# A new order for the pooling mixer and the entry of the second feed-forward network

## The chip, the cores and the metric

The kernel runs on one core of a Trainium2 chip. The core has a matrix engine (TensorE, PE in the profile), a vector engine (VectorE, DVE), an activation engine (ScalarE, ACT), GpSimd (POOL) and SyncE (SP), which issues transfers. Each engine executes its own list of instructions in the order in which the program wrote them and waits on semaphores of the others. The metric is the device time of one launch in microseconds.

## The reference

Two layers of a streaming trunk run over 32 sample tokens and 512 prompt tokens that share weights, in float32. Layer 0 is an attention and recurrence mixer, layer 1 a pooling mixer, and each is followed by a SwiGLU feed-forward network (FFN).

```python
def swiglu(x, w_gate, w_up, w_down):
    return (jax.nn.silu(x @ w_gate) * (x @ w_up)) @ w_down
...
def pool_mixer(xn, buf, start_pos, pool_w, pool_scale):
    b, t, _ = xn.shape
    xcat = jnp.concatenate([buf.astype(xn.dtype), xn], axis=1)
    xf = xcat.astype(jnp.float32)
    cs = jnp.concatenate([jnp.zeros((b, 1, D_MODEL), jnp.float32), jnp.cumsum(xf, axis=1)], axis=1)
    pos = start_pos + jnp.arange(t)
    outs = []
    for gi, win in enumerate(POOL_WINDOWS):
        sl = slice(gi * POOL_GROUP, (gi + 1) * POOL_GROUP)
        end = cs[:, POOL_BUF + 1:POOL_BUF + 1 + t, sl]
        begin = cs[:, POOL_BUF + 1 - win:POOL_BUF + 1 - win + t, sl]
        cnt = jnp.minimum(win, pos + 1).astype(jnp.float32)[None, :, None]
        outs.append((end - begin) / cnt - xf[:, POOL_BUF:, sl])
    d = jnp.stack(outs, axis=2)
    y = jnp.einsum('btgc,gcd->btgd', d, pool_w.astype(jnp.float32)).reshape(b, t, D_MODEL)
    y = y * pool_scale.astype(jnp.float32)
    return y.astype(xn.dtype), xcat[:, -POOL_BUF:]
...
        x = x + y
        x = x + swiglu(rmsnorm(x, norm_ffn[layer]), ffn_gate[layer], ffn_up[layer], ffn_down[layer]).astype(x.dtype)
```

D_MODEL is 1024, the hidden width D_FF 2816, the pooling windows are 2, 4, 8 and 16 tokens, and 15 normalised tokens of history are kept.

## The kernel before

**Layout.** The residual x stays in SBUF with features on the partitions: 8 tiles of 128 features by 544 tokens, used as two halves of 272 tokens (`HALVES`). A float32 product is three matmuls of split operands: high by high, high by low, low by high. So each weight block and each activation tile is first split into a high part (an ACT copy) and a low part (a DVE subtraction).

**FFN.** The hidden width is done in 11 pairs of 128-wide blocks (`PAIRS`). A pair is a Strassen-like scheme (`strassen`): 7 products, each for gate and up, so 14 steps, instead of 8; its right sides are the forms b11, n1, n2, t3, b21, t4 and b22 of the normalised x (sums and differences of feature and token halves), its left sides sums of weight blocks. `beat.tick` counts steps, and `beat.later(n, f)` issues f n steps on. `last_down` multiplies the last hidden blocks by the down weights, adds to x tile by tile and calls `after0(m)`, which makes the mixer's split copies of tile m. The first pair of the second FFN is the exception: it is computed by `plain`, without Strassen, so that it needs only tile k of x and weight blocks a11, a12, a21 and a22 for its step `mm(i, us, k)`; `gate_out` and `up_out` close it.

**Pooling mixer.** `into(t, i)` multiplies token block t (six of them) by the pooling weights of half i of the features into a PSUM bank (12 matmuls). `mid` scales such a bank by the token's 1/rms `rt` into `ptm` (or `pts` for the last block, the 32 sample tokens), by turns on ACT and DVE. `pool_out(m)` applies the window as a banded matrix with 12 matmuls into two PSUM banks and has DVE add both to tile m of x. `pool_hist` prepares the history of the sample stream (a transposition, a DVE copy `hist`, 16 matmuls, two ACT copies into `pts`), `pool_state` writes the new history out (`so`).

**Forms of the second FFN.** `LateForms.add(m)` makes tile m's high parts and its square on ACT; the DVE part (`low`: two low parts, the square added to `nacc`) is issued at the next tile. After all eight tiles `sums()` makes the forms n1, n2, t3 and t4 in ten pieces. `scales` sums the squares over the partitions (`rs`) and takes the root, `n3.out` spreads 1/rms over the partitions through PE and an ACT copy (L204).

**Weights.** `Supply` holds a list of loads, splits and additions with due times in beats; `ahead` issues what is due while slots are free, `need(n)` issues the list up to the block n. Loads go through SP's queue, second summands of weight sums through POOL's.

**Order.** PE, DVE, ACT and SP run exactly in program order here. PSUM has two banks each of `sm` (function `small`) and `z`, and four of `one`.

Of the kernel before, what the change touches and what calls it, by code (L numbers as in the profile page):

```python
# [31 lines left out]
def kernel(  # L32
# [174 lines left out]
    class Norm:  # L207
# [24 lines left out]
        def add(self, k):  # L232
            self.split(k)
            self.square(k)
# [84 lines left out]
    class LateForms(Forms):  # L319
# [10 lines left out]
        def tmp2(self, i):  # L330
            return [hp.tile([P, T], F32R if i > 3 else F32, tag=f"h{p}{i}", name=nm("tmp")) for p in "hl"]

        def add(self, k):

            g = col(self.gcol + k)
            bs = [(x[:, k, s], *self.block(k, h)) for h, s in HALVES]
            for src, h, _ in bs:
                ac.activation(h, src, AF.Copy, scale=g)
            t = self.acc if k == 0 else s2.tile([P, T + NS], F32, tag="nsq", name=nm("nsq"), bufs=1)[:, :T]
            ac.activation(t, x[:, k], AF.Square)  # L340

            def low():
                for src, h, l in bs:
                    ve.scalar_tensor_tensor(l, src, g, h.bitcast(F32), op0=ALU.mult, op1=ALU.subtract)
                if k:
                    ve.tensor_add(self.acc, self.acc, t)

            return low

        def sums(self):  # L350
            g = lambda k: col(self.gcol + k)
            two = lambda t: t.rearrange("p (j c) -> p j c", j=2)
            d, t, q = [[two(b) for b in self.tmp2(i)] for i in range(3)]
            J = range(4)
            at = lambda b, j: b[j // 2][:, j % 2]

            def high(n, i, src):
                ac.activation(self.form(n)[0][:, 2 * i : 2 * i + 2], src, AF.Copy, scale=-1.0)

            def low(n, i, src):  # L360
                h, l = [b[:, 2 * i : 2 * i + 2] for b in self.form(n)]
                ve.scalar_tensor_tensor(l, src, -1.0, h.bitcast(F32), op0=ALU.mult, op1=ALU.subtract)

            def n1(j):
                ac.activation(self.form("n1")[0][:, j], at(d, j), AF.Copy, scale=g(j))
                ac.activation(at(t, j), x[:, 4 + j, HN:], AF.Copy, scale=g(4 + j))

            def n1_low(j):
                h, l = [b[:, j] for b in self.form("n1")]
                ve.scalar_tensor_tensor(l, at(d, j), g(j), h.bitcast(F32), op0=ALU.mult, op1=ALU.subtract)  # L370

            def value(out, a, sc, b, op):
                ve.scalar_tensor_tensor(out, a, sc, b, op0=ALU.mult, op1=op)

            out = []
            for i in range(2):
                def diff(i=i):
                    ve.tensor_tensor(d[i], x[:, 2 * i : 2 * i + 2, :HN], x[:, 2 * i : 2 * i + 2, HN:], op=ALU.subtract)
                    n1(2 * i)
                    n1(2 * i + 1)  # L380
                out.append(diff)
            for i in range(2):
                out.append(lambda i=i: [n1_low(j) for j in (2 * i, 2 * i + 1)])
            for vals, n, b in (
                (lambda j: value(at(q, j), at(d, j), g(j), at(t, j), ALU.add), "n2", q),
                (lambda j: value(at(d, j), x[:, j, HN:], g(j), at(t, j), ALU.subtract), "t3", d),
                (lambda j: value(at(q, j), x[:, 4 + j, :HN], g(4 + j), at(q, j), ALU.subtract), "t4", q),
            ):
                for i in range(2):
                    def both(i=i, vals=vals, n=n, b=b):  # L390
                        vals(2 * i)
                        vals(2 * i + 1)
                        high(n, i, b[i])
                    out.append(both)
                for i in range(2):
                    out.append(lambda i=i, n=n, b=b: low(n, i, b[i]))
            return out


    warm = accp()  # L400
# [452 lines left out]
    class Supply:  # L853
# [93 lines left out]
            self.split(10, n("t4"), n("t4"))  # L947

        def plain(self, fp):
            for j, (t0, t1) in enumerate(((-20, -12), (-18, -10), (-6, 2), (-2, 5))):  # L950
                n = f"a{j // 2 + 1}{j % 2 + 1}", fp
                self.blocks(t0, n, (2 * fp + j // 2, j % 2))
                self.split(t1, n, n)
# [278 lines left out]
    def pool_hist(i):  # L1232
        pw, hraw = pool["w"], pool["hraw"]
        if not i:
            ph = small()
            pe.transpose(ph[:, :120], hraw[:120, :P], ident[:120, :120])
            ve.tensor_copy(hist, ph[:, :120].rearrange("p (t k) -> p k t", k=KD))
            ptb.append(slot("pts"))
# [28 lines left out]
    queues = {ET.PE, ET.DVE, ET.Activation, ET.SP}  # L1267
    with tc.manual_schedule(engines=queues):
        ffn(supply, n1[0], after0, {(0, 3): lambda: scales(n1[0]), (0, 7): lambda: n1[0].out(), **{(2 * g + 2, 4): lambda g=g: bands(g) for g in range(4)},
                                    (PAIRS - 1, 7): pool_load}, lambda: [pool_hist(i) for i in range(2)])  # L1270


    n2 = n2[0]
# [38 lines left out]
    low = []  # L1312

    def pool_out(m):
        g, i = m // 2, m // 4
# [12 lines left out]
        for h, pp in enumerate((pa, pb)):  # L1328
            xs = x[:, m, h * HN : (h + 1) * HN]
            ve.scalar_tensor_tensor(xs, pp[:, :HN], col(40 + m), xs, op0=ALU.mult, op1=ALU.add)  # L1330
        if low:
            low.pop()()
        low.append(n3.add(m))

    with tc.manual_schedule(engines=queues):
        supply = Supply(1, plain=True)
        for _ in range(2):
            supply.ops.pop(0)[2]()
        banks = {}
# [18 lines left out]
        into(3, 1)  # L1358
        mid((2, 1))
        into(4, 1)  # L1360
        pool_out(1)
        mid((3, 1))
        into(5, 1)
        pool_out(2)
        mid((4, 1), (5, 1))
        supply.need(("a12", 0))
        pool_out(3)
        first = {}
        mm, gate_out, up_out = plain(supply, n3, first)
        for m in range(4, KD + 4):  # L1370
            if m < KD:
                pool_out(m)
                if m in (4, 6):
                    pool_state(m == 6)
                if m == 7:
                    give(*ptm, *ptb)
            elif low:
                low.pop()()
                sums = n3.sums()
            beat.tick(supply)  # L1380
            mm(0, (0, 1), m - 4, lambda: one("f0"))
            if m == KD + 3:
                sums.pop(0)()
                sums.pop(0)()
        for k in range(KD):
            if k % 2 == 0:
                beat.tick(supply)
            mm(1, (0,), k, lambda: small("z"))
            sums.pop(0)()
            if k == 2:  # L1390
                scales(n3)
        n3.out()
        for k in range(KD):
            if k % 2 == 0:
                beat.tick(supply)
            if k == 1:
                gate_out(0)
            if k == 4:
                up_out(0)
            mm(1, (1,), k, small)  # L1400
            if sums:
                sums.pop(0)()
        gate_out(1)
        beat.later(3, lambda: up_out(1))

# [98 lines left out]
```

## Time and profile before

| what | us |
|---|---|
| median of 3 runs (1083.84 to 1087.59) | 1085.4 |
| the profiled execution | 1085.57 |
| its span in the trace | 1083.9 |
| PE busy with matmuls (96% of the span) | 1042.1 |
| DVE busy (70%) | 760.1 |
| ACT busy (45%) | 488.8 |
| POOL busy (19%) | 205.5 |

The mean granted clock of TensorE is 0.984 of full speed. A position in the trace is counted in us from the span's start; the end of the first FFN, the pooling mixer and the plain pair of the second FFN lie between 613 and 724. In rows a bracket says how long the engine was idle before, and what released it.

### The profile page before, as it was taken

What the parts mean: (1) busy time and instruction counts of PE and PEld (TensorE: products, weight loads), DVE (VectorE), ACT (ScalarE), POOL (GpSimd) and SP (SyncE); (2) the same over time, 40 slices, a digit from 0 to 9 for tenths busy, and PEclk for the clock granted to TensorE, in tenths of its full rate; (3) what the DMA queues carried; (4) which work ended last, traced back from release to release, by engine and by line L of the source; (5) the groups of instructions that cost most, each with busy time, mean ns of one, the idle gap of its engine ahead of it and who ended that gap; (6) DMA issues with size and microseconds to landing.
All of it is one profiled execution on the core that took longest, in us unless ns stands there. A gap on an engine that the chain in (4) does not pass through costs nothing.

```text
span 1083.9 us, 19767 instructions
## 1 busy us (share of the span) xinstructions
PE 1042.1 (96%) x7995; PEld 1001.6 (92%) x7995; DVE 760.1 (70%) x1222; ACT 488.8 (45%) x814; POOL 205.5 (19%) x327
## 2 busy tenths in 40 slices
PE   7979999999899999999999999879999999999997
PEld 7978888899899999999999898879999999999986
DVE  6776665767788776767766664878867766677653
ACT  7555554544544444433443344564424434244432
POOL 5162225101611111101010101101101111010100
PEclk9989999999999999999999999889999999999999
DMA  8412213423787467665586313336755676656702
GB/s 225 142 51 69 69 42 110 101 59 89 144 188 153 91 136 175 157 143 118 112 172 156 117 31 68 83 79 148 156 118 123 137 175 148 134 128 118 212 3 83
DMA packets 207787, 129.08 MB, mean 119 GB/s; under 512 B 7127, under 2 KB 192703, under 8 KB 207696
## 3 DMA queue, kind: packets, MB, share of 16 engines
q1 hardware_dynamic: 161472, 102.58, 33.4%
q0 software_dynamic: 45584, 24.11, 17.1%
q8 instruction: 63, 1.03, 0.4%
q10 hardware_dynamic: 640, 1.12, 0.3%
q14 instruction: 28, 0.23, 0.1%
HBM read 123.19 MB, written 4.60 MB: 118 GB/s over the span
## 4 chain that ended last, share of the span: by engine, by line
PE 77%; DVE 9%; issue 5%; ACT 4%; DMA 2%; POOL 2%; ACTq 0%; SPq 0%; DVEq 0%; POOLq 0%
PE xy L1054 28%; PE sm L1115 17%; PE z L1054 11%; PE acc L168 10%; PE ps L1137 2%; DVE la L903 2%; ACT ha L902 1%; DVE sB L554 1%; PE pi L1292 1%; DMA rt<-in_ffn_up_dram 1%; DMA sB<-in_x_prompt_dram 1%; PE sm L1016 1%; POOL sA L573 1%; ACT y L1445 1%; DVE y L1451 1%
## 5 line engine op out<-in xcount | busy, mean ns | idle before, releaser
L1115 PE MATMUL sm<-hh,h 128*128 128x272 f32 x576 | 167.5, 291 | 0.8
L1115 PE MATMUL sm<-hl,h 128*128 128x272 f32 x576 | 165.6, 288 | 0.0
L1115 PE MATMUL sm<-hh,l 128*128 128x272 f32 x576 | 165.5, 287 | 0.0
L916 POOL DMA_DIRECT2D rt<-in_ffn_gate_dram x42 | 54.4, 1296 | 574.9 <-DMA rt<-in_ffn_gate_dram 341.5
L903 DVE TENSOR_TENSOR lt<-rt,ht 128x1024 fp32r<-128x1024 f32 x84 | 103.0, 1227 | 46.9 <-ACT ht L902 46.7
L1115 PEld LDWEIGHTS sm<-hh,h 128*128 128x128 f32 x576 | 108.4, 188 | 4.3 <-DVE x L1118 4.3
L1115 PEld LDWEIGHTS sm<-hh,l 128*128 128x128 f32 x576 | 108.4, 188 | 0.0
L1115 PEld LDWEIGHTS sm<-hl,h 128*128 128x128 f32 x576 | 108.4, 188 | 0.0
L98 ACT ACTIVATE s<-s 128x544 f32<-128x544 f32 x44 | 29.0, 659 | 173.3 <-DVE s L1063 171.0
L903 DVE TENSOR_TENSOR la<-ra,ha 128x1024 fp32r<-128x1024 f32 x67 | 82.0, 1226 | 26.2 <-ACT ha L902 26.2
L1054 PE MATMUL xy<-b,ha 128*128 128x272 f32 x672 | 98.3, 289 | 0.8 <-DVE x L758 0.8
L902 ACT ACTIVATE ht<-rt 128x1024 fp32r<-128x1024 f32 x84 | 88.2, 1050 | 5.5 <-DMA rt<-in_ffn_up_dram 3.2
L1054 PEld LDWEIGHTS xy<-b,ha 128*128 128x128 f32 x672 | 89.6, 188 | 1.0 <-DVE x L758 1.0
L1118 DVE TENSOR_TENSOR x<-x,sm 128x272 f32<-128x272 f32 x160 | 69.2, 433 | 28.9 <-PE sm L1115 27.9
L168 PE MATMUL acc<-xh,whi 128*128 128x272 f32 x320 | 75.0, 316 | 2.2 <-ACT xh L98 2.2
L916 POOL DMA_DIRECT2D rt<-in_ffn_up_dram x42 | 74.8, 1781 | 1.5 <-DMA rt<-in_ffn_up_dram 0.8
L999 ACT ACTIVATE hh<-u 128x544 fp32r<-128x544 f32 x44 | 29.0, 658 | 95.3 <-DVE u L1085 48.2
L168 PE MATMUL acc<-xl,whi 128*128 128x272 f32 x320 | 68.1, 294 | 0.8 <-DVE xl L228 0.8
L902 ACT ACTIVATE ha<-ra 128x1024 fp32r<-128x1024 f32 x67 | 68.6, 1051 | 0.0
L168 PE MATMUL acc<-xh,wlo 128*128 128x272 f32 x320 | 67.7, 293 | 0.0
L168 PEld LDWEIGHTS acc<-xh,whi 128*128 128x128 f32 x320 | 50.2, 192 | 9.3 <-issue 5.7
L1072 ACT ACTIVATE c<-xy 128x272 f32<-128x272 f32 x42 | 16.7, 398 | 87.4 <-PE xy L1054 87.4
(423 smaller groups left out, 2552.3 us busy)
## 6 DMA issues: line engine op xcount, KB each, us to landing
r<-in_ffn_down_dram SPq DMA_DIRECT2D x44, 512.0 KB, 5.6
ra<-in_ffn_gate_dram SPq DMA_DIRECT2D x67, 256.0 KB, 5.7
ra<-in_ffn_up_dram SPq DMA_DIRECT2D x67, 256.0 KB, 6.1
rt<-in_ffn_gate_dram SPq DMA_DIRECT2D x42, 256.0 KB, 3.2
rt<-in_ffn_up_dram SPq DMA_DIRECT2D x42, 256.0 KB, 4.1
rt<-in_ffn_gate_dram POOLq DMA_DIRECT2D x42, 256.0 KB, 5.8
rt<-in_ffn_up_dram POOLq DMA_DIRECT2D x42, 256.0 KB, 7.4
raw<-in_hyb_w_in_dram SPq DMA_DIRECT2D x20, 512.0 KB, 3.7
```

What stands on the lines that cost most here:

```text
L98: i = ac.activation(*a, **k).ins
L168: pe.matmul(ps[:, h, : s.stop - s.start], lhsT=a[:, wi, :], rhs=b[:, s], start=first and j == 0, stop=last and j == 2)
L554: ve.tensor_tensor_scan(r, r, r, 1.0, op0=ALU.mult, op1=ALU.min)
L902: ac.activation(hi, raw, AF.Copy)
L903: ve.tensor_tensor(lo, raw, hi.bitcast(F32), op=ALU.subtract)
L916: gp.dma_start(v(t)[:, u], w, accum_op=ALU.add)
L999: beat.later(n, lambda: ac.activation(a, t, AF.Copy))
L1054: pe.matmul(o, lhsT=lt, rhs=r, start=first and n == 0, stop=n == 11, skip_group_check=True)
L1072: ac.activation(pc, o, AF.Copy)
L1115: pe.matmul(ps, lhsT=lt[:, c], rhs=r[:, s], start=i == 0 and j == 0, stop=i == len(fs) - 1 and j == 2)
L1118: ve.tensor_add(xs, xs, ps)
L1137: pe.matmul(o, lhsT=lt[:, c], rhs=r[:, s], start=i == 0 and j == 0, stop=i == len(fs) - 1 and j == 2, skip_group_check=True)
```

## The change

No arithmetic is added or removed on PE, whose instructions are the same in another order. First, the history's transposition and its copy come before product 12 of the last pair; the 16 matmuls stay behind product 13. Second, the splits of weight blocks a11, a12, a21 and a22 are due earlier: a11's and a12's are issued ahead of the mixer's first `into`, a21's and a22's among the mixer's blocks. Third, `mid` takes the first half's blocks in the order 3, 4, 0, 1, 2, 5, and `pool_state` comes at tiles 1 and 2 with a bank of `one`. Fourth, `mm(0, ...)` of the plain pair follows each `pool_out` from tile 3 on. Fifth, the forms are made tile by tile: `after(n, f)` puts a piece n tiles later, `due()` issues what has come up; the squares have two buffers of their own by turns, and n2, t3 and t4 come piece by piece (`sum`) in a loop of 11 steps, in whose step 2 `scales` stands and in step 4 `n3.out`.

```diff
-        def add(self, k):
+        def add(self, k, at):
...
-            t = self.acc if k == 0 else s2.tile([P, T + NS], F32, tag="nsq", name=nm("nsq"), bufs=1)[:, :T]
-            ac.activation(t, x[:, k], AF.Square)
+            sq = self.acc if k == 0 else hp.tile([P, T], F32, tag=f"h{'hl'[k % 2]}0", name=nm("nsq"))
+            ac.activation(sq, x[:, k], AF.Square)
...
-            return low
-
-        def sums(self):
+            at(1, low)
+            if k < 4:
+                h, l = [b[:, j] for b in self.form("n1")]
+                at(1, lambda: ve.tensor_tensor(d, x[:, k, :HN], x[:, k, HN:], op=ALU.subtract))
+                at(2, lambda: ac.activation(h, d, AF.Copy, scale=gk))
+                at(3, lambda: ve.scalar_tensor_tensor(l, d, gk, h.bitcast(F32), op0=ALU.mult, op1=ALU.subtract))
+            else:
+                at(1, lambda: ac.activation(t, x[:, k, HN:], AF.Copy, scale=gk))
+
+        def sum(self, n, i, at):
...
+            at(0, value)
+            at(1, lambda: ac.activation(h, o, AF.Copy, scale=-1.0))
+            at(2, lambda: ve.scalar_tensor_tensor(l, o, -1.0, h.bitcast(F32), op0=ALU.mult, op1=ALU.subtract))
...
-            for j, (t0, t1) in enumerate(((-20, -12), (-18, -10), (-6, 2), (-2, 5))):
+            for j, (t0, t1) in enumerate(((-20, -12), (-18, -10), (-9, -5), (-8, -4))):
...
-                                    (PAIRS - 1, 7): pool_load}, lambda: [pool_hist(i) for i in range(2)])
+                                    (PAIRS - 1, 7): pool_load,
+                                    (PAIRS - 1, 12): lambda: pool_hist(0)}, lambda: [pool_hist(i) for i in (1, 2)])
...
-        pq = small()
+        pq = one("pq")
...
-        if low:
-            low.pop()()
-        low.append(n3.add(m))
+        due()
+        n3.add(m, after)
...
+        supply.need(("a12", 0))
+        for _ in range(2):
+            supply.ops.pop(0)[2]()
...
-        mid(*[(t, 0) for t in range(6)])
+        mid(*[(t, 0) for t in (3, 4, 0, 1, 2, 5)])
+        supply.need(("a21", 0))
         into(1, 1)
         into(2, 1)
         mid((0, 1), (1, 1))
-        pool_out(0)
...
+        supply.need(("a22", 0))
+        for m in range(KD):
+            pool_out(m)
+            if m < 3:
+                into(m + 3, 1)
+                mid((m + 2, 1))
+                if m:
+                    pool_state(m - 1)
+            else:
+                if m == 3:
+                    mid((5, 1))
+                    first = {}
+                    mm, gate_out, up_out = plain(supply, n3, first)
+                beat.tick(supply)
+                mm(0, (0, 1), m - 3, lambda: one("f0"))
+        give(*ptm, *ptb)
+
+        n3.sum("n2", 0, lambda n, f: after(n + 1, f))
+        n3.sum("n2", 1, lambda n, f: after(n + 3, f))
+        for i, n in enumerate(("t3", "t3", "t4", "t4")):
+            n3.sum(n, i % 2, lambda n, f, i=i: after((5, 6, 10, 12)[i] + n, f))
+        after(6, lambda: gate_out(0))
+        after(9, lambda: gate_out(1))
+        after(9, lambda: up_out(0))
+        for m in range(11):
+            if m == 2:
+                scales(n3)
+            if m == 4:
+                n3.out()
+            due()
             beat.tick(supply)
...
+            if m < 3:
+                mm(0, (0, 1), 5 + m, lambda: one("f0"))
+            else:
+                for k in range(2 * m - 6, 2 * m - 4):
+                    mm(1, (k // 8,), k % 8, small if k > 7 else lambda: small("z"))
```

The first place is PE's list at the end of the last pair of the first FFN. The z products are products 12 and 13, `ident,hraw` is the transposition of the history, and `pw,hist` its matmuls. Before:

```order
L1054 MATMUL xy_7043<-t_459_2967,la_1032_7162 128x272 x4
L1054 MATMUL z_7058<-b_461_2971,ht_1035_7195 128x272 x8
L1054 MATMUL z_7058<-b_461_2971,lt_1036_7196 128x272 x4
L1054 MATMUL z_7078<-b_461_2971,ht_1035_7195 128x272 x8
L1054 MATMUL z_7078<-b_461_2971,lt_1036_7196 128x272 x4
L1236 MATMUL sm_7404<-ident,hraw 128x120 [waits DMASW5_49,DVE_49]
L1241 MATMUL sm_7408<-pw_7215,hist 15x256 [waits DMASW2_49,DVE_49]
L1241 MATMUL sm_7408<-pw_7215,hist 15x256
```

And now:

```order
L1037 MATMUL xy_7043<-t_459_2967,la_1032_7162 128x272 x4
L1219 MATMUL sm_7370<-ident,hraw 128x120 [waits DMASW5_49,DVE_49]
L1037 MATMUL z_7058<-b_461_2971,ht_1035_7195 128x272 x8
L1037 MATMUL z_7058<-b_461_2971,lt_1036_7196 128x272 x4
L1037 MATMUL z_7078<-b_461_2971,ht_1035_7195 128x272 x8
L1037 MATMUL z_7078<-b_461_2971,lt_1036_7196 128x272 x4
L1227 MATMUL sm_7408<-pw_7215,hist 15x256 [waits DMASW2_49,DVE_49]
L1227 MATMUL sm_7408<-pw_7215,hist 15x256
```

The transposition has moved ahead of both products, so that one product pair stands between it and the first matmul that needs its copy.

The second place is ACT's list around tile 3 of the pooling mixer. L338 rows are high parts of a tile of x (`b`, `tmp`), L340 its square, L1300 (L1287 now) a `mid`, and L902 the high part of a weight block (`ha`). Before:

```order
L338 ACTIVATE b_1120_7880<-x,cols 128x272 [waits DVE_49]
L338 ACTIVATE tmp_7957<-x,cols 128x272 [waits DVE_49]
L340 ACTIVATE nsq_7961<-x 128x544 [waits DVE_49]
L1300 ACTIVATE ptm_7717<-pi_7901,rt_7814 63x512 [waits PE_49]
L902 ACTIVATE ha_1135_7965<-ra_1105_7721 128x1024 [waits DMAHW1_49,DMAHW0_49]
L902 ACTIVATE ha_1137_7969<-ra_1106_7724 128x1024 [waits DMAHW3_49,DMAHW2_49]
L338 ACTIVATE b_1120_7880<-x,cols 128x272 [waits DVE_49]
L338 ACTIVATE tmp_7957<-x,cols 128x272 [waits DVE_49]
L340 ACTIVATE nsq_7988<-x 128x544 [waits DVE_49,Activation_49]
L338 ACTIVATE b_1146_8005<-x,cols 128x272 [waits DVE_49]
```

And now:

```order
L338 ACTIVATE b_1130_7902<-x,cols 128x272 [waits DVE_49]
L338 ACTIVATE tmp_7986<-x,cols 128x272 [waits DVE_49]
L340 ACTIVATE nsq_7990<-x 128x544
L1287 ACTIVATE ptm_7717<-pi_7948,rt_7828 63x512
L1294 ACTIVATE so_8011<-pq_8006,rt_7828 30x512 [waits PE_49]
L356 ACTIVATE n_1140_7915<-tmp_7909,cols 128x272 [waits DVE_49]
L338 ACTIVATE b_1130_7902<-x,cols 128x272 [waits DVE_49]
L338 ACTIVATE tmp_7986<-x,cols 128x272 [waits DVE_49]
L340 ACTIVATE nsq_8033<-x 128x544 [waits Activation_49]
L1287 ACTIVATE pts_7407<-pi_7992,rt_7828 32x512
```

The two weight splits are gone from here, a `so` copy and n1 pieces have come in, and the copy `pts` of the last `mid`, which DVE did before, stands behind the high parts and the square of tile 3.

The third place is ACT's list where 1/rms of the second FFN is made. L358 rows (L379 now) are high parts of the forms n2 and t3, L98 is the root, L204 and L205 the spread 1/rms `rs`. Before:

```order
L358 ACTIVATE n_1190_8260<-tmp_8158 128x544 [waits DVE_49]
L92 ACT_TABLE_LOAD
L98 ACTIVATE rt_8271<-sm_8265,eps 128x4 [waits PE_49,Activation_49]
L98 ACTIVATE rt_8271<-sm_8265,eps 32x1
L92 ACT_TABLE_LOAD
L358 ACTIVATE n_1190_8260<-tmp_8159 128x544 [waits DVE_49]
L358 ACTIVATE t_1196_8313<-tmp_8154 128x544 [waits DVE_49]
L358 ACTIVATE t_1196_8313<-tmp_8155 128x544 [waits DVE_49]
L204 ACTIVATE rs_8263<-sm_8325 128x512 [waits PE_49]
L205 ACTIVATE rs_8263<-sm_8326 128x32 [waits PE_49]
```

And now:

```order
L885 ACTIVATE ha_1189_8202<-ra_1163_8043 128x1024 [waits DMAHW3_49,DMAHW2_49]
L379 ACTIVATE n_1183_8190<-tmp_7913 128x544 [waits DVE_49]
L92 ACT_TABLE_LOAD
L98 ACTIVATE rt_8239<-sm_8233,eps 128x4 [waits PE_49]
L98 ACTIVATE rt_8239<-sm_8233,eps 32x1
L92 ACT_TABLE_LOAD
L885 ACTIVATE ht_1194_8248<-rt_1162_8038 128x1024 [waits DMASW5_49,DMASW4_49]
L379 ACTIVATE n_1183_8190<-tmp_7914 128x544 [waits DVE_49]
L204 ACTIVATE rs_8231<-sm_8281 128x512 [waits PE_49]
L205 ACTIVATE rs_8231<-sm_8282 128x32 [waits PE_49]
```

The copies of both t3 pieces, which stood ahead of `rs`, have moved behind it, and two splits of the next pair's weights (L885) have come ahead of it.

## Rows read from the trace of the kernel before

**Rows 1.** Page, part 2: the granted clock in 40 slices.

```profile
PEclk9989999999999999999999999889999999999999
```

**Rows 2.** Waits of PE, 724 to 1084: total us, times, longest.

```profile
PE sm L1436 <- DVE hl L996: 0.4, 1, 0.4
```

**Rows 3.** Timeline of PE: start, duration, instruction, and idle time before.

```profile
619.48 1.75 PE L1241 MATMUL sm<-pw,hist 128*15 128x256 f32 x5 [2.36 <-DVE hist L1237]
...
660.92 0.51 PE L1292 MATMUL pi<-pwh,xs 128*128 128x256 f32 x2 [0.69 <-DVE ptm L1298]
...
680.64 0.59 PE L1305 MATMUL sm<-ident,pst 128*30 128x128 f32 x2 [3.83 <-DVE x L1330]
...
710.11 0.62 PE L203 MATMUL sm<-ident,rt 128*128 128x128 f32 x4 [2.44 <-DVE rt L195]
...
715.49 0.82 PE L1016 MATMUL sm<-b,ha 128*128 128x272 f32 x2 [4.60 <-ACT rs L204]
```

**Rows 4.** Windows of PE: busy us, granted clock, DMA share, GB/s.

```profile
620.00:625.00 5.00, 5.00 (x17) 0.66 0.00 0
681.00:685.00 4.00, 4.00 (x21) 0.51 0.02 4
715.50:720.00 4.50, 4.50 (x23) 0.60 0.00 0
```

**Rows 5.** Timeline of DVE before the first and third gap.

```profile
618.15 0.73 DVE L1065 TENSOR_TENSOR s<-s,rs 128x544 f32<-128x544 f32 x1 [0.72 <-ACT s L98]
...
677.32 2.36 DVE L903 TENSOR_TENSOR la<-ra,ha 128x1024 fp32r<-128x1024 f32 x2 [1.59 <-ACT ha L902]
```

**Rows 6.** Timeline of PE: starts of a `pool_out`, and of `mm`, `pool_out`, `mm` in a row.

```profile
668.32 0.38 PE L1327 MATMUL z<-bf,ptm 128*128 128x128 f32 x2
...
689.61 0.50 PE L1016 MATMUL f<-b,ha 128*128 128x272 f32 x2
...
691.19 0.38 PE L1327 MATMUL z<-bf,ptm 128*128 128x128 f32 x2
...
692.73 0.39 PE L1016 MATMUL f<-b,ha 128*128 128x272 f32 x1
```

**Rows 7.** Timeline of DVE, tile 2: from its first addition to the copy behind.

```profile
672.71 0.50 DVE L1330 SCALAR_TENSOR_TENSOR x<-z,cols,x 128x272 f32<-128x272 f32 x1 [1.25 <-PE z L1327]
673.13 0.49 DVE L1330 SCALAR_TENSOR_TENSOR x<-sm,cols,x 128x272 f32<-128x272 f32 x1
...
675.00 0.73 DVE L1298 TENSOR_SCALAR pts<-pi,rt 32x512 f32<-32x512 f32 x1
```

**Rows 8.** Timeline of ACT, tile 1: its first high part, and the copy behind its square.

```profile
670.27 0.52 ACT L338 ACTIVATE b<-x,cols 128x272 fp32r<-128x272 f32 x1 [2.33 <-DVE x L1330]
...
671.66 0.67 ACT L1300 ACTIVATE ptm<-pi,rt 128x512 f32<-128x512 f32 x1
```

**Rows 9.** Timeline of DVE and of PE where the mixer's norm begins.

```profile
654.48 0.43 DVE L1280 COPY na<-nacc 128x15 f32<-128x15 f32 x1
...
657.25 0.28 PE L243 MATMUL sm<-ones,nacc 128*128 128x1 f32 x2
```

**Rows 10.** DMA issues, 616 to 618, then page part 6: to landing.

```profile
ra<-in_ffn_up_dram SPq DMA_DIRECT2D x1, 256.0 KB, 3.4
```

```profile
rt<-in_ffn_up_dram SPq DMA_DIRECT2D x42, 256.0 KB, 4.1
rt<-in_ffn_up_dram POOLq DMA_DIRECT2D x42, 256.0 KB, 7.4
```

**Rows 11.** Two other gaps of PE, and the windows behind them.

```profile
274.85 0.39 PE L1054 MATMUL xy<-n,ht 128*128 128x272 f32 x1 [1.08 <-ACT a L1068]
...
280.45 0.40 PE L1054 MATMUL xy<-t,ht 128*128 128x272 f32 x1 [2.12 <-ACT b L1070]
```

```profile
276.00:280.00 4.00, 2.33 (x17) 1.00 1.07 132
282.00:283.00 1.00, 1.00 (x5) 0.58 0.08 16
```

More of the change, by code (lines that the diff above doesn't have):

```diff
@@ L331, in tmp2 @@
             return [hp.tile([P, T], F32R if i > 3 else F32, tag=f"h{p}{i}", name=nm("tmp")) for p in "hl"]
-        def add(self, k):
-            g = col(self.gcol + k)
+        def add(self, k, at):
+            gk, (j, i) = col(self.gcol + k), (k % 4, k % 4 // 2)
             bs = [(x[:, k, s], *self.block(k, h)) for h, s in HALVES]
             for src, h, _ in bs:
-                ac.activation(h, src, AF.Copy, scale=g)
-            t = self.acc if k == 0 else s2.tile([P, T + NS], F32, tag="nsq", name=nm("nsq"), bufs=1)[:, :T]
-            ac.activation(t, x[:, k], AF.Square)
+                ac.activation(h, src, AF.Copy, scale=gk)
+            sq = self.acc if k == 0 else hp.tile([P, T], F32, tag=f"h{'hl'[k % 2]}0", name=nm("nsq"))
+            ac.activation(sq, x[:, k], AF.Square)
@@ L342, in low @@
             def low():
                 for src, h, l in bs:
-                    ve.scalar_tensor_tensor(l, src, g, h.bitcast(F32), op0=ALU.mult, op1=ALU.subtract)
+                    ve.scalar_tensor_tensor(l, src, gk, h.bitcast(F32), op0=ALU.mult, op1=ALU.subtract)
                 if k:
-                    ve.tensor_add(self.acc, self.acc, t)
-            return low
-        def sums(self):
-            g = lambda k: col(self.gcol + k)
[L352 to L397, printed above, removed]
@@ new lines, in low @@
+                    ve.tensor_add(self.acc, self.acc, sq)
+            if k == 0:
+                two = lambda t: t.rearrange("p (j c) -> p j c", j=2)
+                self.d, self.t, self.q = [[two(b) for b in self.tmp2(n)] for n in (2, 1, 3)]
+            d, t = self.d[i][:, j % 2], self.t[i][:, j % 2]
+            at(1, low)
[6 more added lines that the diff above has]
+                at(1, lambda: ac.activation(t, x[:, k, HN:], AF.Copy, scale=gk))
@@ new lines, in sum, with value @@
+        def sum(self, n, i, at):
+            g = lambda k: col(self.gcol + k)
+            d, t, q = [b[i] for b in (self.d, self.t, self.q)]
+            o = d if n == "t3" else q
+            h, l = [b[:, 2 * i : 2 * i + 2] for b in self.form(n)]
+            def value():
+                for j in range(2):
+                    k = 2 * i + j
+                    if n == "n2":
+                        ve.scalar_tensor_tensor(q[:, j], d[:, j], g(k), t[:, j], op0=ALU.mult, op1=ALU.add)
+                    elif n == "t3":
+                        ve.scalar_tensor_tensor(d[:, j], x[:, k, HN:], g(k), t[:, j], op0=ALU.mult, op1=ALU.subtract)
+                    else:
+                        ve.scalar_tensor_tensor(q[:, j], x[:, 4 + k, :HN], g(4 + k), q[:, j], op0=ALU.mult, op1=ALU.subtract)
+            at(0, value)
+            at(1, lambda: ac.activation(h, o, AF.Copy, scale=-1.0))
+            at(2, lambda: ve.scalar_tensor_tensor(l, o, -1.0, h.bitcast(F32), op0=ALU.mult, op1=ALU.subtract))
@@ L1237, in pool_hist @@
             ve.tensor_copy(hist, ph[:, :120].rearrange("p (t k) -> p k t", k=KD))
+            return
+        i -= 1
+        if not i:
             ptb.append(slot("pts"))
@@ L1311, with after, due @@
     n3 = LateForms(16 + 8, 0)
-    low = []
+    todo = {}
+    def after(n, f):
+        todo.setdefault(step[0] + n, []).append(f)
+    def due():
+        step[0] += 1
+        for f in todo.pop(step[0], []):
+            f()
+    step = [0]
     def pool_out(m):
@@ L1356 @@
         mid((0, 1), (1, 1))
-        pool_out(0)
[L1358 to L1379, printed above, removed]
-            beat.tick(supply)
[L1381 to L1402, printed above, removed]
@@ L1403 @@
-        gate_out(1)
-        beat.later(3, lambda: up_out(1))
+        supply.need(("a22", 0))
[13 more added lines that the diff above has]
+                mm(0, (0, 1), m - 3, lambda: one("f0"))
@@ new lines @@
+        give(*ptm, *ptb)
[12 more added lines that the diff above has]
+            due()
+            beat.tick(supply)
+            if m < 3:
+                mm(0, (0, 1), 5 + m, lambda: one("f0"))
+            else:
+                for k in range(2 * m - 6, 2 * m - 4):
+                    mm(1, (k // 8,), k % 8, small if k > 7 else lambda: small("z"))
@@ L1409 @@
+        beat.later(1, lambda: up_out(1))
+        for n in sorted(todo):
+            for f in todo[n]:
+                beat.later(n - step[0], f)
     TT = [(slice(0, NS), y_s[0])] + [(slice(NS + P * t, NS + P * (t + 1)), y_p[0][P * t : P * (t + 1)]) for t in range(4)]
```

## The prediction

> **What bounds the kernel now.** I read the page's clock row first: full speed almost everywhere, with a dip just past the middle [rows 1]. PE computes for 96% of the span, so only time in which it idles, or runs on the halved clock, can be won. The waits of PE say where that is not: from 724 to the end it waits 0.4 us for anything [rows 2]. The second FFN behind its first pair is therefore a block of fixed length that moves as a whole, and the change can win only what is lost between 613 and 724. There the timeline of PE shows five gaps [rows 3], which I call A to E: 2.36, 0.69, 3.83, 2.44 and 4.60 us, together 13.92. Behind three of them the windows show PE busy without a pause at a mean granted clock of 0.66, 0.51 and 0.60 [rows 4], that is, for a part of the window on the lower of its two levels (1.2 instead of 2.4 GHz). What that cost is the window times what is missing to 1: 5.0 x 0.34 = 1.70 behind A, 4.0 x 0.49 = 1.96 behind C, 4.5 x 0.40 = 1.80 behind D and E, together 5.46. At most 13.92 + 5.46 = 19.4 us are to be had here, and 0.3%, about what a measurement of this kernel can tell from no change, is 3.3.
>
> **Gap A, the history (2.36 + 1.70 = 4.1).** PE waits for DVE's copy `hist`, which stands behind a multiplication by `rs` that itself waits for ACT's silu until 618.15 [rows 3, 5]. Now transposition and copy are issued before product 12. Between them and the first history matmul lie two products, 24 matmuls, some 3 us by the rate of twelve in 1.58 us [rows 6]; the copy is ready in their shadow. I take the whole 4.1. What could eat it is a11's split, which now stands on ACT ahead of the hidden block's copies and waits for its load. In this stretch a load of that kind took 3.4 us [rows 10]; issued as product 13 nears its end, it would hold ACT until about 618. Behind it come the split (about 1) and, by turns on ACT and DVE, the high and low parts of two hidden blocks, four pieces of some 0.7 as the multiplication of [rows 5], with half of them beside each other: ready at about 622 and 624. PE is through with the history at about 620.5 now and wants them as the later blocks of `last_down`'s first group, at about 623.5 and 625, by the 24 matmuls a block that stand ahead of them. So 0 is lost, with some 1 us to spare; these positions are estimates.
>
> **The splits among the mixer's copies.** Two weight blocks cost two ACT copies and two DVE subtractions, of which a pair takes 2.36 us [rows 5]. They fall between the copies for `last_down`, where DVE mostly waits, so I put their delay at about 1.1. The cover is the distance from the end of DVE's last copy for the norm, about 654.9, to the matmul that needs it, 657.25: 2.3 us [rows 9]. Cost 0; without that cover, 1.1.
>
> **Gap B (0.69)** is a bank of PSUM that waits for a DVE copy. With the order 3, 4, 0, 1, 2, 5 that bank's copy is the first on ACT. I take the 0.69.
>
> **Gap C (3.83 + 1.96 = 5.8).** DVE's additions to x, which free the banks, stand behind two weight subtractions of 2.36 us that waited for ACT 1.59 [rows 3, 5]. These splits have moved to places ahead of the tiles, so the gap's cause is gone.
>
> What replaces it is a steady rhythm: `pool_out` 1.54 and one `mm` 1.58, that is 3.12 us of PE for a tile [rows 6]. DVE must keep up. A tile costs it, from the first addition to the end of the `nacc` sum, 2.29, and for tiles 0 to 3 a difference and a low part of n1 more, each half a tile wide like the additions, whose starts lie 0.42 apart [rows 7]: 2.29 + 0.84 = 3.13. That is level, so DVE neither gains nor falls behind by more than hundredths; from tile 4 on it has 0.4 to spare and more.
>
> **A new stall at tile 3.** At its first step `mm` opens four banks of `one`. The fourth is the bank that the last `mid` reads, and its copy into `pts` now stands on ACT behind tile 3's two high parts and square. Let `pool_out(3)` start at 0. In the trace the first high part starts 670.27 - 668.32 = 1.95 after a `pool_out`, and the copy behind the square starts 671.66 - 670.27 = 1.39 later and takes 0.67 [rows 6, 8]: the bank is free at 4.01. PE is there after 1.54 and three of four groups, 1.58 x 3/4 = 1.19, so at 2.73. It waits 1.28, which I book as a loss of 1.3.
>
> Does the clock fall behind such a gap? After 1.08 us it did not (granted clock 1.00), after 2.12 it did (0.58), and behind A's 2.36 too [rows 3, 4, 11]. 1.3 lies nearest to 1.08, so I take no fall; the bound on the other side is the dearest fall seen, 1.96. [...]
>
> **Gaps D and E (2.44 + 4.60 + 1.80 = 8.8).** D waits for the root and its reciprocal, E for ACT's copy `rs`, which came after the high parts of the forms [rows 3], and there was nothing left for PE to do meanwhile. Now the squares are summed at step 2 of the loop, the spread follows at step 4, and PE has products of `mm` in between. Count from the start of `pool_out(7)`: 1.54 + 3 x 1.58 = 6.28 until PE wants the last `nacc` [rows 6]. DVE starts the additions at about 1.4, then has them (0.84), and twice two low parts and a sum (1.45 each, 2.29 less the additions) [rows 7]: 5.1. So there is about 1 us in hand. Between the sum and the spread PE has two steps, 3.16, and the sum, the root and the reciprocal must come in it; I estimate them at 1.7 in all, from the 2.44 that PE waited for them when nothing stood between [rows 3], less the copies that ran ahead of the root. That leaves about 1.5. The copy `rs` is wanted later still. I take the 8.8, and with DVE late by more than these margins D returns.
>
> **Loads.** For the first Strassen pair the last sum of weights (t3) is loaded by SP and POOL once slots come free, at the end of `pool_out(7)`. From there to the first product lie 3 + 8 steps of 1.58, 17.4 us, and t3 is wanted some 9 later. The load needs 4.1, the second summand 7.4 [rows 10], the split about 2. So some 13 stand against 26: cost 0.
>
> **Sum.** 19.4 - 1.3 = 18.1. The profiled execution took 1085.57, so 1067.5; the median of the runs is 0.2 lower than that execution, so I predict 1067.3.
>
> **Rivals.**
> 1. The new gap brings a fall of the clock: 1.3 + 1.7 to 2.0 lost. For it: a gap of 2.12 did. Against: 1.08 did not. 1069.2.
> 2. The new gap does not appear, because the banks come free in time, or the three groups hide it: 1066.0. Against it is only that ACT's order, as it stands in the list, puts the copy last.
> 3. DVE or ACT is late at the seam. The margins are 1 to 1.5 us on a chain of some forty instructions, and DVE has no slack for tiles 0 to 3. Then D's gap comes back with its fall, 2.44 + 1.80 = 4.2: 1071.5. For it: weight splits of 1.2 us each now stand on ACT and DVE just ahead of the root.
> 4. The gain is given back: PE is early, and the second FFN waits where it did not. Its loads on POOL waited for their slots already, and they are released by PE's own progress, so little speaks for it: about 1085, no change.
> 5. Slower: SP's queue is in order, and if one load in it waits for a slot that the new order frees late, pair 1's weights come late as a whole. It costs only what exceeds the 13 us in hand and decides when it exceeds these plus the 18 won, that is, at 31 us late. With 35 the time is about 1089. No load in the trace is near that.
>
> **How the numbers follow.** Forecast 0.5, rival 1 0.2, rival 2 0.1, rival 3 0.15, rival 4 0.03, rival 5 0.02. The forecast with its own blur of 1.5 spans 1065.8 to 1068.8. For 8 in 10 the range needs rivals 1 to 3 and the bounds of the hidden splits (1.1) on the upper side: 1064.5 to 1073.0. Faster by over 0.3% are the first four cases, 0.95; the same 0.03, slower 0.02.
>
> **What would show it.** Right: no wait of PE before the history matmuls and a clock of 1.00 behind them; no wait at the fourth tile's additions; one wait of about 1.3 at the fourth bank of the first `mm`, released by ACT's `pts`; no wait at the reciprocal or `rs`; the first product of the next pair near 724 - 18 = 706. Wrong: a wait on `nacc` or `rt` in the loop, a clock below 1 behind tile 3, hidden parts awaited at the start of `last_down`, or waits for weights behind the first pair.

## The result and the profile after

The changed kernel takes 1068.78 us in the median of 4 runs (1065.23 to 1071.29), the kernel before 1084.85 (4 runs): a ratio of 0.9842 with a 95% interval of 0.9824 to 0.986. The forecast was 1067.3 in a range of 1064.5 to 1073.0. The profiled execution took 1071.29 us with a span of 1068.9. One execution of experiment 4 below ran at a mean granted clock of 0.653 and took 1423.91 us; it is left out of the medians.

Behind 600 PE waits for two things only, and one of them it waited for before [rows 2]. Waits of PE in the changed kernel, 600 to 1068:

```profile
PE f L999 <- ACT pts L1287: 1.1, 1, 1.1
PE sm L1428 <- DVE hl L979: 0.4, 1, 0.4
```

All five gaps of [rows 3] are gone, and a new one has come where the prediction put it, at the fourth bank of `mm`. Timeline of PE, the last low matmuls of product 11, the history's matmuls, the new gap, and the first product of the next pair:

```profile
614.24 0.67 PE L1037 MATMUL xy<-t,la 128*128 128x272 f32 x4
...
617.97 3.62 PE L1227 MATMUL sm<-pw,hist 128*15 128x256 f32 x16
...
673.69 0.54 PE L999 MATMUL f<-tmp,ha 128*128 128x272 f32 x2 [1.12 <-ACT pts L1287]
...
708.35 1.17 PE L1037 MATMUL xy<-b,ha 128*128 128x272 f32 x8
```

The clock stayed up behind the history, as forecast, where [rows 4] had 0.66. But it fell behind the new gap, which the prediction held for the less likely case (rival 1). Windows of PE (busy us, granted clock, DMA share, GB/s):

```profile
620.00:625.00 5.00, 5.00 (x36) 1.00 0.13 39
...
673.00:674.00 1.00, 0.31 (x2) 1.00 0.00 0
674.00:675.00 1.00, 1.00 (x7) 0.52 0.06 16
675.00:676.00 1.00, 1.00 (x6) 0.50 0.00 0
...
680.00:681.00 1.00, 1.00 (x7) 0.56 0.00 0
681.00:682.00 1.00, 1.00 (x9) 1.00 0.00 0
```

Seven windows of 1 us at 0.50 to 0.56, what is missing to 1 added up: 0.48 + 5 x 0.50 + 0.44 = 3.4 us lost behind a gap of 1.1, by the measure of the prediction (experiment 2 gives another).

To compare executions without what happens to the clock in the first 300 us, where it falls behind other gaps, I take one stretch: from the last low matmuls of product 11 of the first FFN's last pair to the first Strassen product of the second FFN. In the kernel before it runs between these rows:

```profile
613.33 0.67 PE L1054 MATMUL xy<-t,la 128*128 128x272 f32 x4
...
723.23 1.17 PE L1054 MATMUL xy<-b,ha 128*128 128x272 f32 x8
```

Before it lasts 723.23 - 613.33 = 109.90 us, in the changed kernel 708.35 - 614.24 = 94.11: 15.8 us are won in it, where the sum said 18.1. The execution entered the stretch 0.9 us late, for reasons ahead of the change. Of the profiled executions of this kernel, of the one before and of experiments 1 to 8, the stretch begins between 612.03 and 615.13, and behind its end the span has 360.5 to 360.7 us left in each. So whole times differ by some 3 us for reasons ahead of the stretch, and medians of four runs have to be read with that in mind.

### The profile page after: what moved, and what is told of

Same layout as the page of the kernel before. It is cut to its first block, busy times and chain, and to the rows that moved or that the text cites. A ratio compares the mean times of both kernels' runs of the same rounds, so it can differ in the third digit from the quotient of the medians.

```text
span 1068.9 us, 19767 instructions
## 1 busy us (share of the span) xinstructions
PE 1038.8 (97%) x7995; PEld 1001.0 (94%) x7995; DVE 758.5 (71%) x1223; ACT 489.0 (46%) x815; POOL 204.2 (19%) x327
## 3 DMA queue, kind: packets, MB, share of 16 engines
q10 hardware_dynamic: 640, 1.12, 0.3%
## 4 chain that ended last, share of the span: by engine, by line
PE 80%; DVE 8%; issue 5%; ACT 3%; DMA 2%; POOL 1%; SPq 0%; ACTq 0%; DVEq 0%; POOLq 0%
PE xy L1037 29%; PE sm L1098 18%; PE z L1037 11%; PE acc L168 11%; PE ps L1120 2%; DVE sB L537 1%; PE f L999 1%; PE pi L1279 1%; DVE la L886 1%; ACT ha L885 1%; DMA raw<-in_hyb_w_in_dram 1%; PE z L1324 1%; POOL sA L556 1%; DMA rt<-in_ffn_up_dram 1%; DVE y L1443 1%
## 5 line engine op out<-in xcount | busy, mean ns | idle before, releaser
L98 ACT ACTIVATE s<-s 128x544 f32<-128x544 f32 x44 | 29.0, 659 | 173.5 <-DVE s L1046 170.9
L885 ACT ACTIVATE ht<-rt 128x1024 fp32r<-128x1024 f32 x84 | 88.3, 1051 | 8.2 <-DMA rt<-in_ffn_up_dram 4.4
L885 ACT ACTIVATE ha<-ra 128x1024 fp32r<-128x1024 f32 x67 | 68.7, 1051 | 4.5 <-DMA ra<-in_ffn_up_dram 4.5
```

Source lines behind the costliest of these rows:

```text
L98: i = ac.activation(*a, **k).ins
L885: ac.activation(hi, raw, AF.Copy)
```

## The experiments

Each ran beside the kernel before on the same chip. "Stretch" is the one just defined, in the profiled execution.

**1. The new gap taken away.** The copy `pts` is made one tile earlier, and so on DVE.

```diff
-                mid((m + 2, 1))
+                mid((m + 2, 1), *[(5, 1)] * (m == 2))
...
-                    mid((5, 1))
```

> The last mid copy (pts) is issued one tile earlier and so on DVE, ahead of tile 3's additions, where DVE idled 0.69 us. Theory: the changed kernel's only wait behind 613, 1.12 us for ACT's pts copy, vanishes, and with it the clock's fall behind it (3.4 us in the profiled execution): 4.5 us less in that stretch, about 1064 us. Rival: the clock falls there because of the short band matmuls, not the gap; then the wait goes, the granted clock between 674 and 681 stays near 0.5, and only 1.1 us are won, about 1067.7 us.

Measured: 1065.85 us (1065.62 to 1066.32), ratio 0.9817 (0.9804 to 0.9831). PE's one wait behind 600 is that for `hl`, 0.4, and the clock stays up. Windows of PE:

```profile
670.00:675.00 5.00, 5.00 (x40) 1.00 0.07 16
675.00:680.00 5.00, 5.00 (x42) 1.00 0.00 0
```

The copy was free on DVE, which idled ahead of tile 3's additions in the changed kernel. Timeline of DVE, the changed kernel and then this one:

```profile
671.04 0.50 DVE L1327 SCALAR_TENSOR_TENSOR x<-z,cols,x 128x272 f32<-128x272 f32 x1 [0.69 <-PE z L1324]
```

```profile
670.44 0.73 DVE L1285 TENSOR_SCALAR pts<-pi,rt 32x512 f32<-32x512 f32 x1
671.21 0.50 DVE L1327 SCALAR_TENSOR_TENSOR x<-z,cols,x 128x272 f32<-128x272 f32 x1
```

The stretch is 704.03 - 614.40 = 89.63, so 4.48 us shorter than in the changed kernel's first profile, as expected for gap and fall together. The same short matmuls run at full clock without the gap, which speaks against the rival; experiment 2 shows that the gap does not bring the fall each time. The whole time is 1.9 above the expected 1064, which took the cost of a fall seen in one execution off a median. By the medians this version is the fastest of the study.

**2. The changed kernel again,** unchanged, on the same chip.

> The changed kernel unchanged, to see more of its executions beside the others on one chip. Theory: the wait of 1.1 us is there in each, but falls of the clock behind short gaps differ from one execution to the next, in places that the change did not touch too; times spread over some 5 us, and the mean granted clock goes with them in steps of about 0.003 for each fall of some 7 us. Rival: the falls are the same each time; times agree within 0.3 per cent, near 1068.8 us.

Measured: 1067.85 us (1067.02 to 1068.82), ratio 0.9836 (0.9822 to 0.9849). The gap is there again, 1.11 us, and this time no fall follows it. Timeline and windows of PE:

```profile
673.36 0.52 PE L999 MATMUL f<-tmp,ha 128*128 128x272 f32 x2 [1.11 <-ACT pts L1287]
```

```profile
670.00:675.00 5.00, 3.89 (x30) 1.00 0.07 16
675.00:680.00 5.00, 5.00 (x39) 1.00 0.00 0
```

Its stretch is 704.95 - 613.89 = 91.06, within 0.8 of what the sum gave (109.90 - 18.1 = 91.8). So the fall behind this gap comes in some executions of one and the same program. The two profiles price both parts: the fall 94.11 - 91.06 = 3.05 us, somewhat less than the 3.4 counted from windows, and the gap without a fall 91.06 - 89.63 = 1.43 us against experiment 1, that is 0.32 more than its idle time. The medians of experiments 1 and 2 differ by 2.0 us; whether the 0.6 beyond 1.43 is a fall in executions without a profile is not shown. The times spread over 1.8 us here, less than the 5 expected; the 6.1 us of the first series were not seen again with this kernel.

**3. The history alone.** The kernel before, with transposition and copy ahead of product 12.

```diff
+            return
+        i -= 1
+        if not i:
...
+                                    (PAIRS - 1, 12): lambda: pool_hist(0)}, lambda: [pool_hist(i) for i in (1, 2)])
```

> The kernel before with nothing but the history's transposition and copy moved ahead of product 12. Theory: gap A and the clock's fall behind it go, 2.36 + 1.70 = 4.1 us less, about 1081 us, with a granted clock of 1.00 from 620 to 625. Rival: the copies of the last hidden blocks, on ACT and DVE, become the wait at the start of the last down products, and less than 2 us are won.

Measured: 1081.35 us against 1085.59, ratio 0.9961 (0.9947 to 0.9974). Gap A is gone and the other four stay; the window behind it, where [rows 4] had 0.66:

```profile
620.00:625.00 5.00, 5.00 (x37) 1.00 0.03 7
```

4.2 us by the medians, 4.5 in the stretch (105.39), 4.1 by the sum.

**4. The first half of the change.** Experiment 3 with the splits of a11 and a12 ahead of the mixer and the new order of `mid`.

```diff
+        supply.need(("a12", 0))
         for t in range(6):
             into(t, 0)
...
-        mid(*[(t, 0) for t in range(6)])
+        mid(*[(t, 0) for t in (3, 4, 0, 1, 2, 5)])
...
-        supply.need(("a12", 0))
```

> The kernel before with the history moved, the splits of a11 and a12 ahead of the mixer's first blocks, and the new order of mid, but with the forms, the plain pair and the norm in the old order. Theory: 4.1 + 0.7 + 5.8 = 10.6 us less, about 1074.5 us, and gaps D and E (2.4 and 4.6 us) with their fall stay. Rival: the gap at tile 4 stays since DVE's additions are late for another reason than the splits; then about 1080 us.

Measured: 1075.3 us in the median of four runs (1074.58 to 1077.26), ratio 0.9902 (0.9886 to 0.9917). Waits of PE, 600 to 730: gaps B and C are gone, D and E as they were.

```profile
PE sm L1016 <- ACT rs L204: 4.6, 1, 4.6
PE sm L203 <- DVE rt L195: 2.4, 1, 2.4
```

The stretch is 99.99 us, 5.4 less than in experiment 3, where the sum had 0.69 + 5.8 = 6.5. The step from here to experiment 1 is what the rest of the change (forms, plain pair, norm, the splits of a21 and a22, `pool_state`) is worth without the new gap: 9.5 us by the medians, 10.4 in the stretch, 8.8 by the sum. The waits of D and E are what they were, so I put most of the 1.1 less and part of the 1.6 more down to the clock. Windows of PE in experiment 4 at D and E, and the timeline from E to the next pair:

```profile
700.00:705.00 5.00, 0.79 (x5) 0.68 0.00 0
705.00:710.00 5.00, 3.79 (x16) 0.50 0.00 0
710.00:715.00 5.00, 5.00 (x34) 0.80 0.35 104
```

```profile
706.21 0.82 PE L1016 MATMUL sm<-b,ha 128*128 128x272 f32 x2 [4.59 <-ACT rs L204]
...
714.95 1.17 PE L1054 MATMUL xy<-b,ha 128*128 128x272 f32 x8
```

Behind E's gap the windows give 1.9 + 1.0 = 2.9 us lost, against 1.80 before (the matmuls behind D take 0.79 in either trace). The timeline agrees on the difference: the same products last 714.95 - 706.21 = 8.74 us here and 723.23 - 715.49 = 7.74 before, 1.0 more.

**5 and 6. The new gap shorter and longer.** In the changed kernel, `pts` copied on ACT ahead of tile 3's square; and the square made three times, with the same values.

```diff
+            if hook:
+                hook()
             sq = self.acc if k == 0 else hp.tile([P, T], F32, tag=f"h{'hl'[k % 2]}0", name=nm("nsq"))
...
-        n3.add(m, after)
+        n3.add(m, after, (lambda: mid((5, 1))) if m == 3 else None)
```

```diff
-            ac.activation(sq, x[:, k], AF.Square)
+            for _ in range(3 if k == 3 else 1):
+                ac.activation(sq, x[:, k], AF.Square)
```

> The changed kernel with the pts copy on ACT ahead of tile 3's square instead of behind it: 0.55 us earlier. Theory: PE's wait at the fourth bank falls from 1.12 to about 0.55 us, and no execution loses clock there; about 1066.4 us, 0.55 above the kernel without the wait (1065.85). Rival: the wait is set by something else than this copy's place on ACT, and stays at 1.1 us; 1067.9 us.

> The changed kernel with tile 3's square done three times on ACT (same values written again), so that the pts copy comes 1.1 us later. Theory: PE's wait becomes 2.2 us, and at that length the clock falls behind it in every execution (granted clock near 0.5 for some 4 to 7 us, 2 to 3.4 us lost): 1065.85 + 2.2 + 2.0 to 3.4 = about 1070 to 1071.5 us. Rival: the fall is not tied to the gap's length; then the wait alone is added, about 1069 us.

Measured: 1068.66 us (1066.55 to 1069.66) with the shorter gap, 1072.64 (1071.5 to 1073.75) with the longer one. Timeline of PE in either:

```profile
673.99 0.52 PE L1001 MATMUL f<-tmp,ha 128*128 128x272 f32 x2 [0.56 <-ACT pts L1289]
```

```profile
674.58 0.52 PE L1000 MATMUL f<-tmp,ha 128*128 128x272 f32 x2 [2.49 <-ACT pts L1288]
```

The windows behind, first with the shorter gap, then with the longer one:

```profile
675.00:680.00 5.00, 5.00 (x39) 1.00 0.00 0
```

```profile
675.00:680.00 5.00, 5.00 (x24) 0.52 0.02 3
680.00:685.00 5.00, 5.00 (x34) 0.80 0.00 0
```

So the gap goes by the copy's place on ACT, as the prediction said: 0.56, 1.1, 2.49. The stretch with the shorter one is 90.43 us, 0.8 more than without, and its clock does not fall. The longer one has 95.44, that is 5.8 more, about the gap of 2.49 and a fall of 2.4 + 1.0 = 3.4 by the windows. Its whole time is 1.1 above the upper end of what was expected. The whole time of the shorter one is 2.3 us above what was expected, although its stretch is as expected. In its profiled execution the rest lies outside the stretch: it begins at 615.13, 0.7 later than in experiment 1, and the device time exceeds the span by 2.4 us instead of 1.7.

**7. The margin at the norm.** Experiment 1 with the low parts of tiles 6 and 7 made twice on DVE, 1.64 us ahead of the last sum of squares.

```diff
-                for src, h, l in bs:
+                for src, h, l in bs * (2 if k > 5 else 1):
```

> The kernel with pts on DVE, and the low parts of tiles 6 and 7 done twice on DVE (same values), 1.64 us more ahead of the last sum of squares. Theory: the profile's margin there is 0.9 us, so PE waits about 0.7 us for nacc at the sum, and nothing is late behind it: 1065.85 + 0.7 = 1066.6 us. Rival: DVE has more slack than the timeline shows, and nothing changes; or the margin of the reciprocal goes too, and PE waits there as well, with a fall of the clock, 1069 us or more.

Measured: 1067.42 us (1064.86 to 1070.59). Waits of PE, 600 to 730:

```profile
PE sm L243 <- DVE nacc L346: 0.7, 1, 0.7
```

1.64 - 0.7 = 0.9 us of margin, as the timeline of the changed kernel shows it, and no wait behind it. The stretch is 90.60, 1.0 more. As in experiments 2 and 5, a gap without a fall costs more than its idle time: 0.3 more here, 0.32 and 0.24 there. In these traces a matmul of 0.29 us starts 0.125 behind the one before it; idle time counted from a matmul's end leaves out the 0.16 by which it outlasts that, which is about half of the difference by this estimate.

**8. The history put back,** in the kernel of experiment 1.

```diff
-                                    (PAIRS - 1, 7): pool_load,
-                                    (PAIRS - 1, 12): lambda: pool_hist(0)}, lambda: [pool_hist(i) for i in (1, 2)])
+                                    (PAIRS - 1, 7): pool_load}, lambda: [pool_hist(i) for i in range(3)])
```

> The kernel with pts on DVE, and the history's transposition and copy put back behind product 13. Theory: the parts interact. The copy again stands on DVE behind the product with ACT's silu, and the silu now stands behind a11's split, which waits for its load until 618.9; so PE waits about 4.5 us, not 2.4, and with the clock's fall 1.7 to 2 more: about 1072 us, 6.2 above. Rival: the parts are additive, 4.1 above as when the history alone is moved in the kernel before: 1070 us.

Measured: 1072.12 us (1071.12 to 1073.62), 6.3 above experiment 1; the stretch is 96.73 us, 7.1 more. Timeline of PE, and of ACT ahead of the gap's end:

```profile
621.72 6.26 PE L1227 MATMUL sm<-pw,hist 128*15 128x256 f32 x16 [4.39 <-DVE hist L1220]
```

```profile
618.22 1.06 ACT L885 ACTIVATE ha<-ra 128x1024 fp32r<-128x1024 f32 x1 [4.54 <-DMA ra<-in_ffn_up_dram]
...
619.73 0.64 ACT L98 ACTIVATE s<-s 128x544 f32<-128x544 f32 x1
```

4.39 and not the 2.36 of [rows 3], since a11's split now stands ahead of the silu on ACT: the parts of the change are not additive. That a11's split moved forward alone would make gap A longer follows from this order, but was not run.

**9 and 10. Twenty gaps of four lengths.** Experiment 1 with two pauses in each Strassen pair of the second FFN; number 10 exchanges the numbers of copies between the places. Each pause adds two matmuls and some copies whose results nothing uses.

```diff
+    def pause(n, lt, r):
+        o = one("gap")[:, :HN]
+        pe.matmul(o, lhsT=lt, rhs=r, start=True, stop=True)
+        for _ in range(n):
+            ac.activation(scrap, o, AF.Copy)
+        pe.matmul(o, lhsT=lt, rhs=r, start=True, stop=True)
...
+            if sup.l and fp and (i, u) in ((1, 0), (4, 1)):
+                pause((1, 2, 4, 7)[(2 * fp + u) % 4], *mms[0])
```

> The kernel with pts on DVE, and in each Strassen pair of the second FFN two pauses put into PE's list: a matmul, 1, 2, 4 or 7 ACT copies of its bank, and the matmul again, so that PE waits about 0.6, 0.9, 1.5 or 2.4 us (estimates from copies of 0.40 us with starts 0.29 apart), five times each, amid work in which PE never waits otherwise. Theory: whether the clock falls behind a gap goes by its length but not by it alone; of the shortest gaps none is followed by a fall, of those of 1 to 1.5 us some, of those of 2.4 nearly all. Then 27 us of gaps and some 7 falls of 2 to 3.4 us: about 1065.9 + 27 + 19 = 1112 us. Rival: there is one sharp length, the same in each place, below which the clock never falls and above which it always does.

> The same twenty pauses with the numbers of copies exchanged between the places (1 with 2, 4 with 7). Theory: as many falls as before at each length, in other places, about 1112 us. Rival: falls follow the place in the pair and not the length.

Measured: 1154.93 and 1152.0 us. The pauses came out longer than estimated, 0.49 to 5.45 us, in all 53 us instead of 27 in either run, so the total says little; the gaps themselves are what was wanted. Two gaps of one length in number 9, timeline of PE and the 10 us behind each:

```profile
824.86 0.39 PE L1022 MATMUL gap<-n,ht 128*128 128x272 f32 x1 [2.86 <-ACT scrap L1021]
...
909.00 0.59 PE L1022 MATMUL gap<-n,ht 128*128 128x272 f32 x1 [2.86 <-ACT scrap L1021]
```

```profile
824.86:834.86 10.00, 9.96 (x77) 1.00 0.58 102
909.00:919.00 10.00, 10.00 (x67) 0.83 0.58 102
```

And three in number 10, behind gaps of 1.77, 4.93 and 1.77 us:

```profile
730.82:740.82 10.00, 10.00 (x80) 1.00 0.89 179
...
781.89:791.89 10.00, 10.00 (x59) 0.71 0.38 77
806.58:816.58 10.00, 10.00 (x67) 0.83 1.07 235
```

All forty, each judged by the granted clock of the 10 us behind it:

| idle, us | gaps | with a fall | granted clock behind a fall |
|---|---|---|---|
| 0.49 and 0.92 | 10 | 0 | |
| 1.77 | 5 | 4 | 0.83 |
| 2.37 to 2.87 | 6 | 5 | 0.83 to 0.84 |
| 3.06 to 5.45 | 19 | 19 | 0.69 to 0.72, or 0.83 to 0.85 |

Each run has 14 falls, where some 7 were expected. Of the theory the first half holds: length decides much, and not alone. Length and place are mixed in part, since one of the two places had only gaps from 2.37 up. The other place has the clean comparison: no fall behind ten gaps of 0.49 and 0.92, four behind five of 1.77, five behind five of 3.06. The rival of one sharp length falls with the pairs above, since gaps of 1.77 and of 2.86 us were followed by a fall or not. That the place in the pair decides does not fit either, since one place had gaps of 1.77 with a fall and without.

## Why the prediction was right, and where it was off

**What bounds the kernel, and the ceiling.** Right. The second FFN behind its first pair has the same single wait and the same length, 360.5 to 360.7 us in ten profiles, and without any gap (experiment 1) the stretch is 109.90 - 89.63 = 20.3 us shorter, against 19.4 counted; 0.35 of the rest are two short waits that I left out. The sum also left out the 0.3 us or so that a gap costs beyond its idle time, and counted falls by windows, which gave 3.4 where two executions of one program differ by 3.05; these errors are of opposite sign.

**Gap A** was booked at 4.1 and brought 4.2 by the medians when made alone. The margin for the hidden parts held: no wait at the start of `last_down`. That was in part luck, since both sides of it came about 1 us later than estimated: a11's split waited on ACT until 618.90 instead of about 618, and PE was through with the history at 621.52 instead of about 620.5. Timelines of ACT and PE in the changed kernel:

```profile
618.90 1.06 ACT L885 ACTIVATE ha<-ra 128x1024 fp32r<-128x1024 f32 x1 [4.52 <-DMA ra<-in_ffn_up_dram]
```

```profile
621.52 0.39 PE L1120 MATMUL ps<-hh,h 128*128 128x272 f32 x1
```

**Gaps B and C** at 6.5 brought 5.4 in the stretch, and **D and E** at 8.8 brought 10.4, without the new gap; together 15.8 against 15.3. The idle times came out as read. What was mis-sized is the clock's share, which is not the same in every execution: in experiment 4 the fall at E cost 1.0 more than before. Whether that comes of C being gone is not shown.

**The margins at the norm.** I had about 1 us for the last `nacc`; the timeline shows 0.9, and experiment 7 measures it. I had 1.5 for the reciprocal. Timelines of DVE and PE in the changed kernel:

```profile
691.23 0.72 DVE L346 TENSOR_TENSOR nacc<-nacc,nsq 128x544 f32<-128x544 f32 x1
...
695.07 0.29 DVE L195 RECIPROCAL rt<-rt 128x4 f32<-128x4 f32 x2 [1.17 <-ACT rt L98]
```

```profile
692.87 1.10 PE L243 MATMUL sm<-ones,nacc 128*128 128x1 f32 x10
...
697.01 0.77 PE L203 MATMUL sm<-ident,rt 128*128 128x128 f32 x5
```

The sum ends at 691.95 and is wanted at 692.87; the reciprocals, two with starts about 0.2 apart, end near 695.5 and are wanted at 697.01. Rival 3 did not come.

**The new stall** was booked at 1.3 and is 1.1, at the bank and behind the instruction that were named.

**The clock behind it** is the one step that failed in part. The prediction took no fall, because 1.3 lies nearest to the 1.08 us gap of [rows 11]; one execution shows a fall of 3.4 us by windows, above the bound of 1.96 that I took for the dearest fall seen, and another shows none. The row itself was no accident: the same gap, 1.08 to 1.10 us in the ten profiles, has a granted clock of 1.00 behind it in each. But it did not hold for a gap of like length at another place. Nor was 1.96 the dearest fall of the trace, since behind an idle time of 5.38 us at 72 the kernel before lost 0.93 + 1.00 + 0.68 = 2.6. Timeline and windows of PE in the kernel before:

```profile
72.15 1.08 PE L602 MATMUL sm<-ident,k 128*128 128x128 f32 x4 [5.38 <-DVE k L649]
```

```profile
72.00:74.00 2.00, 1.85 (x9) 0.50 0.24 71
74.00:76.00 2.00, 2.00 (x10) 0.50 0.55 146
76.00:78.00 2.00, 2.00 (x14) 0.66 0.85 247
```

The right term was a gap's cost and a chance times a fall's price, not a yes or no from one row. With the prices of experiment 2 the sum gives 1085.4 - 19.4 + 1.43 = 1067.4 without a fall and 1070.5 with one, and the two medians, 1067.85 and 1068.78, lie between; two profiles are too few to give the chance. That the forecast of 1067.3 came within 1.5 us of the median is in part luck: an execution with the fall, like the profiled one, loses 3 us more. The Trainium skill (TensorE: Matmul & The Clock Gate, section "Why this matters for your kernels") advises against idle gaps between bursts of matmuls, since they put the clock back, but only against gaps much longer than 1.12 us. By it no fall was due here; the trace differs in the one profile, by 3.05 us, and agrees in the other, and the measurement decides.

**Rivals 4 and 5** have nothing for them: behind the first pair PE waits 0.4 us, as before.

## What to carry to other kernels

In a kernel whose matrix engine is the bound, list its gaps one by one, add what the clock loses behind each, and take the sum as the ceiling; moving the releasing instruction ahead on its own in-order engine wins it, if the list there is followed to see what the move makes late. A new short gap is priced as its length, here with some 0.3 us on top, plus a chance of a fall times the fall's cost, from several gaps of like length and not from the nearest one. Look for a copy that another engine can make in its own idle time: giving `pts` to DVE took one call moved up and won 2.0 us more by the medians, 1.43 in the stretch against the execution without a fall.

## What the runs showed of the hardware

The same idle time of TensorE, at the same place of the same program, was followed by half clock in one execution (1.12 us idle, 3.05 us lost) and by full clock in another (1.11 us), while a gap of 1.08 to 1.10 at another place had no fall in any of ten profiles. Within one execution five gaps of 1.77 us gave four falls. And falls came in about two sizes, not in the order of the gaps' lengths: by windows, behind the forty gaps a fall cost either 1.5 to 1.7 us or 2.8 to 3.1 us of the next 10, the small price behind gaps as long as 4.41, the large behind 3.06; all nine falls behind gaps of 1.77 to 2.87 had the small price, and all four behind gaps of 4.93 and more the large one. What decides between them is not shown by these runs.
